# Two gate tiles in fp32 from the normalised activations at the head of a hybrid block's input projection, with h made beside them

## The chip, the cores and the metric

The kernel runs on one core of one Trainium2 chip. The metric is the device time of one execution in microseconds (us); lower is better. A profiled execution also has a span, from its first recorded instruction to its last, and the numbers of the trace count from the start of that span.

## The reference, cut to what matters

One layer works on 1024 tokens of width 1024, all in float32:

```python
mod = silu(c) @ ada_w + ada_b                  # 3072 numbers for the one sequence
shift, scale, gate = split(mod, 3)
h = rms_norm(x, norm_w) * (1 + scale) + shift
proj = h @ w_in                                # columns: q,k,v,z,beta,decay | q,k,v,z | g_A,g_B
y_A = (headwise_norm(gated_delta_rule(q, k, v)) * silu(z_A)) @ P_A      # 8 heads, 16 chunks of 64
y_B = (dilated window attention * silu(z_B)) @ P_B                      # 12 heads in 3 groups
x = x + gate * ((sigmoid(g_A) * y_A + sigmoid(g_B) * y_B) @ w_out)
out = rms_norm(x, final_norm_w)
```

With xn for x divided by its root mean square, and A = norm_w * (1 + scale), the first line of the block is h = A * xn + shift. A column w of the input projection is therefore h @ w = xn @ (A * w) + shift @ w. The two forms of this equation are the kernel before and a part of the change.

## The kernel before, in words

Everything on chip is held transposed, with features on the 128 partitions and the 1024 tokens along the free axis. h is eight such tiles (`hT[kk]`, kk from 0 to 7). The program multiplies in two ways. A plain float32 matmul is issued as two instructions. The large products use a split instead: each operand is written as hi + lo in the type float32r, and three products (hi by hi, hi by lo, lo by hi) are added up in PSUM. One output tile of the projection, 128 features by 1024 tokens, so takes 8 kk x 3 products x 2 halves of 512 tokens = 48 matmuls of 128x512.

The order of all instructions is set before the kernel runs. Each piece of work is a Python generator (a stream) with a priority; `Sched.run` steps the streams with a rough clock of its own, and what they issue lands in each engine's queue in that order. On the chip every engine runs its queue strictly in order and waits for what it needs. The projection is the stream of lowest priority (99): it fills TensorE wherever the others wait by that clock. A buffer comes from a pool of slots (`big` has 34 tiles of 128x1024); `get(add=...)` makes a projection tile wait until enough slots are left, so a tile of the attention (kinds qB, add=4) can be held back while the recurrence holds its buffers, where a gate tile (add=0) is not.

The head of the kernel, all before the first steady stretch, is this:

- SyncE (SP) issues the loads in the order of `LOADS`: the eight tiles of x, then pairs of ada_w tiles (scale tile 8+kk with shift tile kk) and the halves of the first two weight tiles.
- `ln_start`: ScalarE squares and sums a tile of x, VectorE adds eps, GpSimd takes the power -0.5, VectorE multiplies the tile by it in place.
- `consts_start` broadcasts c over the partitions with a float32 matmul and applies SiLU, into the SBUF tile `scb[0]`.
- `ada_stream`: for each kk two products with sum on VectorE (`ada_dot`, 128x1024 each, both inputs in SBUF), an addition of the bias, and A_d[kk].
- `h_stream`: for each kk and half, four transposes on TensorE, then two ScalarE passes with scale A_d and bias shift (one to hi, one to a float32 scratch), then on GpSimd lo = scratch - hi.
- `projections`, streams `first`: the first two tiles (k of heads 0 and 1, called k0 and k1 here) take each kk as it comes; all later tiles run whole.

After the head comes the gated delta rule in four pairs of heads. Its recurrence (`rec_stream`) is a serial chain over 8 steps: the state products kt*st and qt*st, VectorE, the product with `tt`, a ScalarE copy, the products kp*w and at*w, VectorE again. The matmuls are 128x128 in plain float32, and two heads run in step. Between them TensorE runs the projection's matmuls. The list `ORDER` says which projection tiles come while which pair runs; a "g" in it takes the next of 16 gate tiles.

```python
    for g_ in range(3):
        for i_ in (0, 1):
            feat("qB", 2 * g_ + i_)
            feat("kB", 2 * g_ + i_)
```

These follow `ORDER`, then six zB tiles, then gate tiles that are left, and then the output products.

Of the kernel before, what the change touches and what calls it, by code (L numbers as in the profile page):

```python
# [21 lines left out]
LOADS = "s x0 s x1 s x2 s x3 x4 x5 x6 x7 a0 w00 w10 a1 a2 a3 w01 a4 a5 a6 a7 w11"  # L22
LAG = 2
FIRST = 2
INFLIGHT = 4
# [25 lines left out]
class Slots:  # L51
# [201 lines left out]
def hybrid_block_kernel(ctx: ExitStack, tc: tile.TileContext, x, c, norm_w, ada_w, ada_b, w_tiles, w_vb0, w_vb1,  # L253
# [82 lines left out]
    def load_start():  # L336
        for u in units[0:FIRST]:
            u.raw = yield from (big if u is units[2] else wr).get(shape=[P, u.n])
            u.half_raw, u.half_ev = [Event(), Event()], [Event(), Event()]
# [3 lines left out]
        for o in LOADS.split():  # L343
# [11 lines left out]
            else:  # L355
                kk = int(o[1])
                if kk >= INFLIGHT:
                    yield ada_ev[kk - INFLIGHT]
                yield from ada_fetch(kk)
# [39 lines left out]
    def consts_start():  # L399
# [7 lines left out]

        for hf in range(2):
            pb = yield from sb.get()
            pe.matmul(pb, one_row, scb[1][0:1, hf * 512:(hf + 1) * 512], start=True, stop=True)  # L410
            yield
            if hf == 0:
                scb[0] = yield from big.get()
            act.activation(scb[0][:, hf * 512:(hf + 1) * 512], pb, AF.Silu)
            sb.put()
        big.put()
        S.set(ev_mod)

    def ln_start():
        junk = yield from big.get()  # L420
        live = [8]

        def one(i):
# [21 lines left out]
    ada_ev = [Event() for _ in range(24)]  # L445

    def ada_dot(j, aw):
        mdt = yield from big.get()
        dve.scalar_tensor_tensor(mdt, aw, 1.0, scb[0], op0=OP.mult, op1=OP.mult, accum_out=mod[:, j:j + 1])
        dve.tensor_tensor(mod[:, j:j + 1], mod[:, j:j + 1], adab[:, j:j + 1], op=OP.add)  # L450
        big.put()

    def ada_stream():
        for kk in range(8):
            yield ev_mod
            for j in (8 + kk, kk):
                yield ev_aw[j]
                yield from ada_dot(j, aw[j])
                big.put()
            dve.scalar_tensor_tensor(A_d[:, kk:kk + 1], mod[:, 8 + kk:9 + kk], 1.0, nw_t[:, kk:kk + 1],  # L460
                                     op0=OP.add, op1=OP.mult)
            S.set(ada_ev[kk])
        yield ev_k[1]
        for j in range(16, 24):
# [3 lines left out]
            yield from ada_dot(j, a_)  # L468
# [5 lines left out]
    todo_h = []  # L474
    for k_ in range(8 + LAG):
        todo_h += [(kk, hf) for hf in range(2) for kk in [k_ - LAG * hf] if 0 <= kk < 8]
    h_left = [16]

    def h_stream():
        while todo_h:  # L480
            kk, hf = todo_h.pop(0)
            h32 = yield from mid.get()
# [5 lines left out]
            yield ada_ev[kk]
            if kk not in hT:
                hT[kk] = None  # L490
                hi = yield from big.get(F32R)
                lo = yield from big.get(F32R)
                hT[kk] = (hi, lo)
            yield lambda: hT[kk] is not None
            hi, lo = hT[kk]
            sl = slice(hf * 512, hf * 512 + 512)
# [32 lines left out]
    def w_split():  # L529
        yield lambda: hasattr(units[FIRST - 1], "half_raw")  # L530
        for u in units[0:FIRST]:
            u.pool = big if u is units[2] else wh
            u.hi = yield from u.pool.get(F32R, shape=[P, u.n])
            u.lo = yield from u.pool.get(F32R, shape=[P, u.n])
        for q in range(2):
            for u in units[0:FIRST]:
                yield u.half_raw[q]
                sl = slice(q * 512, q * 512 + 512)
# [1184 lines left out]
```

## Time and profile before

| | |
|---|---|
| median of 3 runs | 1302.04 us (1301.1 to 1302.54) |
| the profiled execution | 1300.81 us, its span 1299.0 us |
| TensorE (PE) busy | 1261.6 us, 97% of the span |
| VectorE (DVE) busy | 690.9 us, 53% |
| ScalarE (ACT) busy | 494.3 us, 38% |
| GpSimd (POOL) busy | 145.4 us, 11% |
| DMA | 137.65 MB, 106 GB/s on average |

The rows of the trace name an operation by the tiles that it writes and reads: `pj` are the PSUM tiles of the projection, `sb` the small PSUM tiles, `wr` raw weights, `wh` split weights, `mid` scratch of 128x512, `mod` the 24 columns of shift, scale and gate. L96 is the helper that records every instruction, so the rows are told apart by tiles and times. A row of the timeline has its start, its length, engine, operation, out<-in, shapes and how many instructions are merged in it; in brackets stands the idle time before it and what ended that. PEld is TensorE's weight load, which overlaps the matmuls; a plain float32 matmul shows as two instructions in the trace.

### The profile page before, as it was taken

Reading aid. Unit: us, or ns where it says so; the run is one execution under the profiler, and the core shown is the slowest. Engines: PE = TensorE matmul, PEld = TensorE weight load, DVE = VectorE, ACT = ScalarE, POOL = GpSimd, SP = SyncE. Lnnn points to the kernel's source line nnn. Section 1 sums busy time; section 2 is a strip of 40 time slices with the busy share of each in tenths; the row PEclk is TensorE's granted clock in tenths of the full one; section 3 lists DMA queues with packets and bytes.
Section 4 is the critical chain, followed back from the end, with each engine's and each line's share of the span. In section 5 each row is a group of like instructions: output and inputs, shape, how many; then the busy total and the mean of one; then the engine's idle time right before and its main releaser. Section 6 shows DMA issues by size and latency. Waiting matters only on the chain.

```text
span 1299.0 us, 18858 instructions
## 1 busy us (share of the span) xinstructions
PE 1261.6 (97%) x7386; PEld 1049.0 (81%) x7386; DVE 690.9 (53%) x1437; ACT 494.3 (38%) x1054; POOL 145.4 (11%) x97
## 2 busy tenths in 40 slices
PE   5799899999999999999999999999999999999997
PEld 3698678988888988888888888777777888888886
DVE  6766682377763468843778533232322147645433
ACT  5637312455234362234542242453536342222211
POOL 4601200023000221001310002000000000002400
PEclk9899999999999999999999999999999999999999
DMA  9335532163321433231522226211100257333422
GB/s 362 120 123 179 95 93 58 33 197 94 95 70 40 149 125 93 78 102 33 179 74 73 82 66 194 66 35 65 35 33 33 83 187 208 102 127 117 156 95 89
DMA packets 76138, 137.65 MB, mean 106 GB/s; under 512 B 30193, under 2 KB 43921, under 8 KB 76050
## 3 DMA queue, kind: packets, MB, share of 16 engines
q1 hardware_dynamic: 75906, 136.20, 33.2%
q8 instruction: 58, 0.95, 0.3%
q14 instruction: 30, 0.25, 0.1%
q10 hardware_dynamic: 144, 0.26, 0.1%
HBM read 105.84 MB, written 30.59 MB: 105 GB/s over the span
## 4 chain that ended last, share of the span: by engine, by line
PE 82%; issue 7%; DVE 6%; DMA 3%; POOL 1%; ACT 1%; SPq 0%; POOLq 0%; DVEq 0%; ACTq 0%
PE pj L96 69%; PE sb L96 13%; DVE big L96 4%; DMA big<-in_x_dram 1%; DMA vtd<-big 1%; DVE wh L96 1%; POOL big L96 1%; DVE mod L96 1%; DMA big<-grow 0%; ACT big L96 0%; DVE mid L96 0%; DMA big<-otd 0%; SPq L96 0%; POOL mo L96 0%; DMA otd<-big 0%
## 5 line engine op out<-in xcount | busy, mean ns | idle before, releaser
L96 PE MATMUL pj<-big,wh 128*128 128x512 f32 x3840 | 941.8, 398 | 11.2 <-POOL big L96 6.4
L96 PEld LDWEIGHTS pj<-big,wh 128*128 128x128 f32 x3840 | 706.3, 189 | 157.5 <-POOL big L96 7.8
L96 ACT ACTIVATE wh<-wr 128x1024 fp32r<-128x1024 f32 (+3 forms) x96 | 95.6, 996 | 316.1 <-PE pj L96 292.4
L96 DVE TENSOR_TENSOR wh<-wr,wh 128x1024 fp32r<-128x1024 f32 (+3 forms) x93 | 115.5, 1243 | 148.1 <-ACT wh L96 147.9
L96 ACT ACTIVATE big<-big 128x1024 f32<-128x1024 f32 (+1 forms) x61 | 64.5, 1059 | 147.2 <-DVE big L96 115.7
L96 PE MATMUL pj<-wh,big 128*128 128x256 f32 (+2 forms) x702 | 109.5, 307 | 0.0
L96 PEld LDWEIGHTS pj<-wh,big 128*128 128x128 f32 x702 | 95.9, 189 | 5.2 <-DVE big L96 0.2
L96 DVE SCALAR_TENSOR_TENSOR big<-pj,cw,big 128x1023 f32<-128x1023 f32 (+2 forms) x66 | 84.4, 1279 | 1.8 <-ACT big L96 0.3
L96 PEld LDWEIGHTS sb<-sq,big 128*128 128x128 f32 x464 | 62.6, 191 | 4.4
L96 PE MATMUL sb<-sq,big 128*128 128x128 f32 x464 | 65.5, 274 | 0.0
L96 DVE TENSOR_TENSOR big<-big,big 128x1024 f32<-128x1024 f32 (+3 forms) x40 | 55.2, 1388 | 15.1 <-ACT big L96 13.0
L96 ACT ACTIVATE big<-pj 128x1024 f32<-128x1024 f32 (+1 forms) x56 | 51.7, 923 | 21.3 <-PE pj L96 21.2
L96 ACT ACTIVATE mid<-sb 128x384 f32<-128x384 f32 (+5 forms) x75 | 34.1, 461 | 66.8 <-PE sb L96 66.4
L96 POOL TENSOR_TENSOR wh<-wr,wh 128x1024 fp32r<-128x1024 f32 x3 | 8.4, 2785 | 399.0 <-ACT wh L96 399.0
L96 ACT ACTIVATE mid<-mid,sta 128x128 f32<-128x128 f32 (+1 forms) x96 | 42.2, 441 | 25.5 <-DVE sta L96 25.4
L96 DVE COPY big<-sb 128x256 f32<-128x256 f32 (+1 forms) x32 | 12.4, 389 | 74.0 <-PE sb L96 73.9
L96 DVE SCALAR_TENSOR_TENSOR sq<-sq,gsm,sb 128x128 f32<-128x128 f32 x48 | 16.5, 345 | 63.2 <-PE sb L96 61.8
L96 PE MATMUL pj<-big,big 128*128 128x512 f32 x210 | 49.1, 389 | 0.0
L96 ACT ACT_TABLE_LOAD x29 | 37.2, 1283 | 28.8 <-DVE big L96 23.9
L96 PE MATMUL sb<-big,big 128*128 128x128 f32 (+4 forms) x365 | 45.5, 316 | 2.0 <-DVE big L96 2.0
L96 PEld LDWEIGHTS pj<-big,big 128*128 128x128 f32 x210 | 39.4, 188 | 8.2
L96 DVE TENSOR_TENSOR mid<-big 64x31 f32<-64x31 f32 (+15 forms) x124 | 41.1, 332 | 9.0 <-POOL big L96 5.6
(124 smaller groups left out, 1086.3 us busy)
## 6 DMA issues: line engine op xcount, KB each, us to landing
wr<-in_w_tiles_dram SPq DMA_DIRECT2D x64, 512.0 KB, 3.9
big<-in_ada_w_dram SPq DMA_DIRECT2D x24, 512.0 KB, 9.0
big<-in_x_dram SPq DMA_DIRECT2D x16, 512.0 KB, 5.0
gd<-big SPq DMA_DIRECT2D x16, 512.0 KB, 5.0
big<-gd SPq DMA_DIRECT2D x16, 512.0 KB, 4.7
big<-grow SPq DMA_DIRECT2D x8, 512.0 KB, 5.6
vtd<-big SPq DMA_DIRECT2D x8, 512.0 KB, 3.0
big<-vtd SPq DMA_DIRECT2D x32, 128.0 KB, 3.8
```

Source lines behind the costliest of these rows:

```text
L96: r = f(*a, **k)
```

## The change

The list of tiles begins with two gate tiles (`gA` 0 and 1, called g0 and g1 here) instead of k0 and k1; k0 and k1 come third and fourth, as ordinary split tiles. Two gate tiles fewer are left for `ORDER` and the end. g0 and g1 are computed in plain float32 from xn: the transposed xn is kept in SBUF (`XT`, a ScalarE copy of the transposes), the raw weights are multiplied by A_d on GpSimd (`u.ws`), and each tile is 16 float32 matmuls of 128x512 instead of 48 split ones. shift enters as sixteen matmuls with one column (`mod` against the raw weights), whose result is the bias `fb` of the tanh. The loads bring the eight scale tiles (e0 to e7) first and the eight shift tiles (f0 to f7) behind them. silu(c) now stays in PSUM for the sixteen dots, which are one custom VectorE instruction with the bias added in. h is made from XT: hi by one ScalarE pass of 1024, the float32 values by two VectorE passes of 512, lo on GpSimd as before.

```diff
-LOADS = "s x0 s x1 s x2 s x3 x4 x5 x6 x7 a0 w00 w10 a1 a2 a3 w01 a4 a5 a6 a7 w11"
+LOADS = "s x0 s x1 s x2 s x3 w00 w10 e0 e1 x4 e2 x5 e3 x6 w01 e4 w11 x7 e5 e6 e7 f0 f1 f2 f3 f4 f5 f6 f7"
-INFLIGHT = 4
+INFLIGHT = 5
...
     def consts_start():
...
+        pb = yield from pj.get()
         for hf in range(2):
-            pb = yield from sb.get()
-            pe.matmul(pb, one_row, scb[1][0:1, hf * 512:(hf + 1) * 512], start=True, stop=True)
...
+            pe.matmul(pb[:, hf * 512:hf * 512 + 512], one_row, scb[1][0:1, hf * 512:hf * 512 + 512], start=True, stop=True)
+        yield
+        act.activation(pb, pb, AF.Silu)
+        scb[2] = pb
+        S.set(ev_mod)
+        yield
+        scb[0] = yield from big.get()
+        act.activation(scb[0], pb, AF.Copy)
...
     def ada_dot(j, aw, cc):
         mdt = yield from big.get()
-        dve.scalar_tensor_tensor(mdt, aw, 1.0, scb[0], op0=OP.mult, op1=OP.mult, accum_out=mod[:, j:j + 1])
-        dve.tensor_tensor(mod[:, j:j + 1], mod[:, j:j + 1], adab[:, j:j + 1], op=OP.add)
+        dve.tensor_tensor_reduce(mdt, aw, cc, 1.0, adab[:, j:j + 1], op0=OP.mult, op1=OP.add, accum_out=mod[:, j:j + 1])
...
+        for n, j in enumerate([8, 9, 10, 11, 12, 13, 14, 15, 0, 1, 2, 3, 4, 5, 6, 7]):
+            yield ev_aw[j]
+            yield from ada_dot(j, aw[j], scb[2])
...
+            if n < 8:
+                dve.tensor_scalar(A_d[:, n:n + 1], mod[:, j:j + 1], 1.0, nw_t[:, n:n + 1], op0=OP.add, op1=OP.mult)
...
+    def xt_stream():
...
+            for i in range(4):
+                pe.transpose(pb[:, i * P:(i + 1) * P], xs[4 * hf + i][:, kk * P:(kk + 1) * P], ident)
...
+            act.activation(XT[kk][:, hf * 512:hf * 512 + 512], pb, AF.Copy)
...
     def h_stream():
...
-            act.activation(hi[:, sl], pb, AF.Identity, bias=mod[:, kk:kk + 1], scale=A_d[:, kk:kk + 1])
-            act.activation(h32, pb, AF.Identity, bias=mod[:, kk:kk + 1], scale=A_d[:, kk:kk + 1])
...
-            pool.tensor_tensor(lo[:, sl], h32, hi[:, sl].bitcast(F32), op=OP.subtract)
+            act.activation(hi, XT[kk], AF.Identity, bias=mod[:, kk:kk + 1], scale=A_d[:, kk:kk + 1])
+            for q in range(2):
+                sl = slice(q * 512, q * 512 + 512)
+                dve.tensor_scalar(ts[q], XT[kk][:, sl], A_d[:, kk:kk + 1], mod[:, kk:kk + 1], op0=OP.mult, op1=OP.add)
+            yield
+            for q in range(2):
+                sl = slice(q * 512, q * 512 + 512)
+                pool.tensor_tensor(lo[:, sl], ts[q], hi[:, sl].bitcast(F32), op=OP.subtract)
...
+    def first_weights():
...
+            for u in units[0:FIRST]:
+                pool.tensor_tensor(u.ws[:, ks], u.raw[:, ks], A_d[:, kk:kk + 1].to_broadcast([P, P]), op=OP.mult)
+            S.set(ev_ws[kk])
+        yield ev_sh
+        pb = yield from sb.get()
+        for q, u in enumerate(units[0:FIRST]):
+            for kk in range(8):
+                pe.matmul(pb[:, q:q + 1], u.raw[:, kk * P:kk * P + P], mod[:, kk:kk + 1], start=kk == 0, stop=kk == 7)
+        wh.put(2)
+        yield
+        dve.tensor_scalar(fb, pb[:, 0:2], 0.5, None, op0=OP.mult)
...
+    gate_tile()
+    gate_tile()
     feat("kA", 0)
     feat("kA", 1)
...
         def first(q, hf):
...
-                pe.matmul(o, u.hi[:, ks], hi[:, sl], start=kk == 0, stop=False)
-                pe.matmul(o, u.hi[:, ks], lo[:, sl], start=False, stop=False)
-                pe.matmul(o, u.lo[:, ks], hi[:, sl], start=False, stop=kk == 7)
+                pe.matmul(o, u.ws[:, kk * P:kk * P + P], XT[kk][:, sl], start=kk == 0, stop=kk == 7)
```

How this moves instructions is shown at three places. The first is TensorE's queue at the end of the head. Before, it goes from the last split matmuls of k1 (`pj_235`) straight to the third tile, q of head 0 (`pj_634`, weights `wh_559` and `wh_560`):

```order
L96 MATMUL pj_235<-big_519,wh_231 128x512
L96 MATMUL pj_235<-big_547,wh_230 128x512
L96 MATMUL pj_235<-big_548,wh_230 128x512
L96 MATMUL pj_235<-big_547,wh_231 128x512
L96 MATMUL pj_634<-big_304,wh_559 128x512 x2
L96 MATMUL pj_634<-big_305,wh_559 128x512 x2
```

With the change, g0 is `pj_224`, the second half of g1 is `sb_227`, and the third tile, `pj_596`, is k0. `sb_531` is the product for the bias, and it reads all eight shift columns of `mod`:

```order
L103 MATMUL pj_224<-big_342,wh_221 128x512
L103 MATMUL pj_224<-big_347,wh_221 128x512
L103 MATMUL sb_227<-big_263,wh_222 128x512
L103 MATMUL sb_531<-mod,wh_183 128x1 x8
L103 MATMUL sb_531<-mod,wh_184 128x1 x8
L103 MATMUL sb_227<-big_268,wh_222 128x512
L103 MATMUL sb_227<-big_287,wh_222 128x512
L103 MATMUL sb_227<-big_290,wh_222 128x512
L103 MATMUL sb_227<-big_315,wh_222 128x512
L103 MATMUL sb_227<-big_321,wh_222 128x512
L103 MATMUL sb_227<-big_342,wh_222 128x512
L103 MATMUL sb_227<-big_347,wh_222 128x512
```

The bias product stands ahead of the last seven float32 matmuls of g1 and of k0, which come right behind it.

The second place is VectorE's queue around the last shift dots of the change. A row "ISA" is the dot (f5, f6 and f7 here, each followed by its sum into `mod`); the rows into `mid` are the float32 values of h for kk = 3 (`big_290`), 4 and 5:

```order
L103 ISA big_488,mod<-big_409,pj_228,adab 128x1024
L103 ISA mod 128x1
L103 TENSOR_SCALAR mid_492<-big_290,A_d,mod 128x512
L103 TENSOR_SCALAR mid_493<-big_290,A_d,mod 128x512
L103 ISA big_499,mod<-big_428,pj_228,adab 128x1024
L103 ISA mod 128x1
L103 ISA big_502,mod<-big_453,pj_228,adab 128x1024
L103 ISA mod 128x1
L103 TENSOR_SCALAR mid_508<-big_315,A_d,mod 128x512
L103 TENSOR_SCALAR mid_509<-big_315,A_d,mod 128x512
```

Eight of the sixteen passes into `mid` (kk = 0 to 3) stand ahead of the last dot, and eight behind it.

The third place is TensorE's queue in the last steps of the recurrence of the last pair of heads (`TT_100`, `TT_101`; `sb<-sq` are the state products). Before, every step has projection matmuls between its parts:

```order
L96 MATMUL sb_6792<-sq_6782,TT_101 128x128
L96 MATMUL pj_6711<-big_451,wh_6307 128x512 x2
L96 MATMUL sb_6796<-sq_6787,TT_100 128x128
L96 MATMUL pj_6711<-big_452,wh_6307 128x512 x2
L96 MATMUL sb_6804<-sq_6798,big_5725 128x128
L96 MATMUL sb_6804<-sq_6798,big_5543 128x128
L96 MATMUL sb_6807<-sq_6802,big_5621 128x128
L96 MATMUL sb_6807<-sq_6802,big_5454 128x128
L96 MATMUL pj_6711<-big_451,wh_6308 128x512 x2
L96 MATMUL pj_6711<-big_481,wh_6307 128x512 x2
L96 MATMUL sb_6821<-sq_6810,big_5538 128x128
L96 MATMUL sb_6821<-sq_6810,big_6044 128x128
```

With the change, the same step of the same two heads reads:

```order
L103 MATMUL sb_6833<-sq_6827,TT_101 128x128
L103 MATMUL sb_6835<-sq_6830,TT_100 128x128
L103 MATMUL sb_6841<-sq_6837,big_5792 128x128
L103 MATMUL sb_6841<-sq_6837,big_5610 128x128
L103 MATMUL sb_6844<-sq_6839,big_5688 128x128
L103 MATMUL sb_6844<-sq_6839,big_5521 128x128
L103 MATMUL sb_6854<-sq_6847,big_5605 128x128
L103 MATMUL sb_6854<-sq_6847,big_6111 128x128
L103 MATMUL sb_6858<-sq_6850,big_5516 128x128
L103 MATMUL sb_6858<-sq_6850,big_5694 128x128
```

Three steps in a row are without any projection matmul there. In this stretch 52 of 62 projection matmuls are gone, and 4 of them come back in the block behind it; the other 48 that leave the later part of the queue stood in the long run of projection and output matmuls ahead of and in the output products. Between the head and this stretch the queue keeps its order, apart from blocks whose ends shift by two to four matmuls, and behind it too.

More of the change, by code (lines that the diff above doesn't have):

```diff
@@ L70, in get, with many @@
         return self.pool.tile(shape or self.shape, dtype, tag=self.tag, name=f"{self.tag}{self.count}")
+    def many(self, n):
+        yield lambda: len(self.free_at) >= n
+        ts = []
+        for _ in range(n):
+            ts.append((yield from self.get()))
+        return ts
     def put(self, n=1, t=None):
@@ L355, in load_start @@
             else:
[L356 to L359, printed above, removed]
+                n, j = len(aw), int(o[1]) + (8 if o[0] == "e" else 0)
+                if n >= INFLIGHT:
+                    yield ev_dot[n - INFLIGHT]
+                aw[j] = yield from big.get()
+                restart()
+                sp.dma_start(aw[j], ada_w[j * P:(j + 1) * P, :])
+                S.set(ev_aw[j])
         ev_loaded.t = S.now()
@@ L472, in ada_stream @@
         big.put()
[L474 to L482, printed above, removed]
+    todo_x = [(kk, hf) for hf in range(2) for kk in range(8)]
+    x_left = [8, 8]
+    def xt_stream():
+        while todo_x:
+            kk, hf = todo_x.pop(0)
             yield [ev_ln[hf], ev_const]
@@ L486, in h_stream @@
                 pe.transpose(pb[:, i * P:(i + 1) * P], xs[4 * hf + i][:, kk * P:(kk + 1) * P], ident)
+            x_left[hf] -= 1
+            if not x_left[hf]:
+                big.put(4)
             yield
[L488 to L495, printed above, removed]
@@ L496, in h_stream @@
[L496 to L498 removed]
+            if kk not in XT:
+                XT[kk] = None
+                XT[kk] = yield from big.get()
+            yield lambda: XT[kk] is not None
+            act.activation(XT[kk][:, hf * 512:hf * 512 + 512], pb, AF.Copy)
             sb.put()
[L500 removed]
@@ L529, in w_split @@
     def w_split():
[L530 to L538, printed above, removed]
-                act.activation(u.hi[:, sl], u.raw[:, sl], AF.Copy)
-                yield
-                dve.tensor_tensor(u.lo[:, sl], u.raw[:, sl], u.hi[:, sl].bitcast(F32), op=OP.subtract)
-                S.set(u.half_ev[q])
-                if q:
-                    (big if u is units[2] else wr).put()
         for u in units[FIRST:]:
@@ L636, in hybrid_block_kernel, with first_out @@
     GT = {}
+    def first_out(q, j, pt):
+        t = GT[j]
+        for hf in range(2):
+            act.activation(t[:, hf * 512:hf * 512 + 512], pt[hf], AF.Tanh, bias=fb[:, q:q + 1], scale=0.5)
+        (pj if q < 1 else sb).put(1 + q)
+        yield
+        sp.dma_start(gate_d[j], t)
+        S.set(ev_gate[j])
+        big.put()
     prog = []
```

119 lines of the change are left out of this document (66 added, 53 removed).

## The prediction

> **What bounds the kernel now.** I read the page first, its busy times and slices.
>
> ```profile
> PE 1261.6 (97%) x7386; PEld 1049.0 (81%) x7386; DVE 690.9 (53%) x1437; ACT 494.3 (38%) x1054; POOL 145.4 (11%) x97
> PE   5799899999999999999999999999999999999997
> ```
>
> TensorE is the bound from the third slice on; 37 us of idle are left, and the first two slices hold most. So I cut the trace into stretches (stretch, length, then busy of PE, PEld, DVE, ACT, POOL, the granted clock, DMA share, GB/s).
>
> ```profile
> 0.00:22.00 22.00, 9.00 (x20) 4.25 (x20) 10.55 (x28) 13.54 (x23) 8.74 (x16) 1.00 0.91 341
> 22.00:44.00 22.00, 15.99 (x71) 11.94 (x71) 21.65 (x36) 12.50 (x19) 14.59 (x8) 1.00 0.88 332
> 44.00:66.00 22.00, 18.54 (x75) 14.60 (x76) 12.27 (x19) 13.41 (x19) 12.83 (x9) 0.84 0.13 38
> 100.00:200.00 100.00, 93.28 (x456) 77.50 (x455) 71.78 (x162) 40.38 (x77) 14.04 (x8) 0.98 0.46 121
> 700.00:800.00 100.00, 100.00 (x710) 84.65 (x709) 49.94 (x107) 34.97 (x90) 8.33 (x5) 1.00 0.30 89
> ```
>
> From 22 to 44 us VectorE is busy 21.65 of 22 us, so it paces the head, with the loads (332 GB/s) ahead of it; later on TensorE has no gap, as from 700 to 800 us. The timeline shows how the head ends.
>
> ```profile
> 47.89 1.21 DVE L96 SCALAR_TENSOR_TENSOR big<-big,big 128x1024 f32<-128x1024 f32 x1
> 49.03 0.07 DVE L96 DVE_READ_ACCUMULATOR big<-big,big 128x1 f32 x1
> 49.14 1.12 DVE L96 TENSOR_TENSOR mod<-mod,adab 128x1 f32<-128x1 f32 x1
> 53.88 0.15 DVE L96 SCALAR_TENSOR_TENSOR A_d<-mod,nw_t 128x1 f32<-128x1 f32 x1
> 55.63 2.63 POOL L96 TENSOR_TENSOR big<-mid,big 128x512 fp32r<-128x512 f32 x2 [1.70 <-ACT mid L96]
> 76.58 14.45 PE L96 MATMUL pj<-wh,big 128*128 128x272 f32 x114
> ```
>
> The last scale column is ready at 53.88, lo follows on GpSimd, and the fourth tile of the program (values, 128x272 products) begins at 76.58: then k0, k1 and q of head 0, three tiles, are done. **My sum compares this instant with the one at which g0, g1 and k0 are done.** Behind it both queues hold the same number of projection matmuls in almost the same order.
>
> **The change part by part.** First the prices.
>
> ```profile
> 1252.21 0.55 POOL L96 TENSOR_TENSOR fss<-fss,pw 128x1 f32<-128x1 f32 x1 [10.33 <-DVE fss L96]
> 1263.09 0.55 POOL L96 TENSOR_TENSOR fss<-fss,pw 128x1 f32<-128x1 f32 x1 [10.33 <-DVE fss L96]
> 312.06 3.57 PE sb L96 x32
> 109.82 0.78 PE L96 MATMUL sb<-gsm,cst 128*128 128x64 f32 x6
> 163.92 0.25 PE L96 MATMUL sb<-qpart,cst 128*32 128x8 f32 x8 [4.74 <-DVE qpart L96]
> L96 DVE CUSTOM_DVE_ANT_0 mid<-sb,cst 128x256 f32<-128x256 f32 x44 | 17.4, 420 | 8.3 <-PE sb L96 8.2
> L96 DVE CUSTOM_DVE_ANT_0 mid<-sb,cst 128x128 f32<-128x128 f32 x52 | 13.2, 288 | 15.5 <-PE sb L96 15.5
> L96 DVE TENSOR_SCALAR big<-big,rstd 128x1024 f32<-128x1024 f32 x8 | 6.0, 753 | 4.0 <-POOL rstd L96 4.0
> L96 POOL TENSOR_TENSOR big<-mid,big 128x512 fp32r<-128x512 f32 x16 | 27.4, 1720 | 15.5 <-ACT mid L96 15.4
> 1196.40 2.41 POOL L96 TENSOR_TENSOR big<-wr,big 128x1024 fp32r<-128x1024 f32 x1 [4.99 <-PE pj L96]
> 1196.44 1.22 DVE L96 SCALAR_TENSOR_TENSOR big<-big,pj 128x1024 f32<-128x1024 f32 x1 [1.53 <-PE pj L96]
> 1197.70 2.20 DVE L96 TENSOR_TENSOR big<-big,big 128x1024 f32<-128x1024 f32 x1
> ```
>
> A split tile of 48 matmuls takes 1263.09 - 1252.21 = 10.9 us. Sixteen plain float32 matmuls of 128x128 take 3.57 us, 0.223 each, so one of 128x512 about 0.9 (estimate, four times the columns), and a gate tile 16 x 0.9 = 14.4 us. The two dearer tiles alone would lose 2 x (14.4 - 10.9) = 7.0 us; the gain must come from starting earlier.
>
> *Dot.* The custom instruction with one PSUM input grows by 132 ns per 128 elements: 288 + 7 x 132 = 1.21 us at 1024, and with its sum I take a pitch of 1.3. The bias addition of the old form (1.12 above, mostly waiting) is gone. A VectorE instruction with a PSUM input ran its 1.22 us in full beside a GpSimd one (1196.44 against 1196.40), while one with two SBUF inputs then took 2.20. So I let the dots run free beside lo. [...]
>
> *Start.* The fourth tile of x was normalised from 12.49 to 13.24.
>
> ```profile
> 5.41 1.06 ACT L96 ACTIVATE big<-big 128x1024 f32<-128x1024 f32 x1 [0.34 <-DMA big<-in_x_dram]
> 6.37 0.19 ACT L96 ACTIVATION_READ_ACCUMULATOR big<-big 128x1 f32 x1
> 10.32 1.06 ACT L96 ACTIVATE big<-big 128x1024 f32<-128x1024 f32 x1 [0.16 <-DMA big<-in_x_dram]
> 12.49 0.75 DVE L96 TENSOR_SCALAR big<-big,rstd 128x1024 f32<-128x1024 f32 x1 [0.66 <-POOL rstd L96]
> 2.40 3.75 PE L96 MATMUL sb<-big,one_row 1*128 1x512 f32 x4 [2.40 <-DMA big<-in_c_dram]
> ```
>
> Now ScalarE's SiLU waits for both broadcast matmuls (2.40 + 3.75 = 6.15) and takes about 1.1 in one piece, so the first square starts near 7.4 instead of 5.41. A square with its sum takes 1.15 (5.41 to 6.56), and a copy of 1.0 stands between them, so the fourth starts at 7.4 + 3 x 1.15 + 1.0 = 11.85 instead of 10.32, and the normalisation ends 1.5 later: 14.7.
>
> *Scale phase.* VectorE does 8 dots (10.4), 8 A_d (0.8), four normalisations (4 x 0.75) and their small parts (0.6), and I add 0.6 of waits: 15.4, ending at 30.1. The loads cover this: e7 is complete at 9.5 MB, and at the rates above 7.5 MB are in by 22 us, so it lands at 22 + 2.0 / 0.332 = 28.0.
>
> *Shift phase, to the last dot.* 8 dots are 10.4; the eight passes of 512 ahead of it cost, by 753 ns for 1024, between 0.38 and 0.75 each; I take 0.45, 3.6. Each may wait for a running lo, between nothing and 1.3 (half of the 2.63 for two lo at 55.63); I take 0.45, 3.6. End: 30.1 + 17.6 = 47.7. f7 lands at 40.7 (13.7 MB), so nothing waits for the loads.
>
> *TensorE behind it.* Ahead of the bias it has 25 float32 matmuls (22.5) and 64 transposes (at 0.11, 7.1) from about 16.6 on, when the first dot and its weights are through: 46.2. So it **waits about 1.5 us for the bias**, with seven matmuls of g1 and all of k0 queued behind. Sixteen one-column products are 32 instructions, between 0.03 (163.92: 8 in 0.25) and 0.13 each (109.82: 6 in 0.78); I take 0.06, 1.9 us. Then 7 x 0.9 = 6.3 and k0's 10.9: 47.7 + 19.1 = 66.8.
>
> ```profile
> 44.55 1.17 PE L96 MATMUL pj<-big,wh 128*128 128x512 f32 x2 [2.28 <-POOL big L96]
> 46.22 2.48 PE L96 MATMUL pj<-big,wh 128*128 128x512 f32 x6
> 37.79 1.64 PE L96 MATMUL pj<-big,wh 128*128 128x512 f32 x6
> ```
>
> After an idle of 2.28 six matmuls took 2.48 instead of 1.64 us, so I add 1.0: **67.8, and the head gains 76.6 - 67.8 = 8.8 us.** [...]
>
> *lo on GpSimd.* Sixteen lo at the mean of 1.72 take 27.5 from about 35: 62.5. k0 needs the last one near 66.4, so they are covered by 3.9 us; beyond that k0 waits for lo one for one. The sixteen products for `u.ws` (128x128, about 0.4 by a quarter of lo) lie in the scale phase, where GpSimd is mostly idle. ScalarE loses 32 passes of 512 and gains 16 copies of 512 and 8 passes of 1024, and it was busy 12.5 of 22 us: no cost. k0's weights are loaded behind f7 and split on ScalarE and VectorE (1.2 each) beside g1's last matmuls; the bytes loaded stay the same.
>
> *The recurrence without its filler.* A full step of both heads today:
>
> ```profile
> 770.45 1.06 PE L96 MATMUL sb<-sq,big 128*128 128x128 f32 x8
> 771.17 0.73 DVE L96 SCALAR_TENSOR_TENSOR sq<-sb,gsm,big 128x128 f32<-128x128 f32 x2 [0.89 <-PE sb L96]
> 772.27 0.38 PE L96 MATMUL sb<-sq,TT 128*128 128x128 f32 x2
> 772.69 0.28 ACT L96 ACTIVATE sq<-sb 128x128 f32<-128x128 f32 x1 [0.38 <-PE sb L96]
> 773.64 1.05 PE L96 MATMUL sb<-sq,big 128*128 128x128 f32 x8
> 774.28 0.35 DVE L96 SCALAR_TENSOR_TENSOR sq<-sq,gsm,sb 128x128 f32<-128x128 f32 x1 [2.38 <-PE sb L96]
> 777.27 0.38 PE L96 MATMUL sb<-sq,TT 128*128 128x128 f32 x2
> ```
>
> It is 5.0 long (772.27 to 777.27), full of TensorE work: ten recurrence matmuls (2.3) and twelve fillers (2.7). Bare, only the chain counts: 0.72 to VectorE, 0.36 there, 0.42 to ScalarE, 0.28 there, 0.64 to VectorE, 0.35 there, and about 0.1 for each return to TensorE: 3.0. TensorE idles 3.0 - 2.3 = 0.7 in each of three bare steps, with the half-bare ends about **3.0 us lost** (nearer 1 if the hops overlap better, 10.9 = 48 x 0.227 if a bare step stays at 5.0).
>
> *Sum:* -8.8 + 3.0 = -5.8, so the profiled execution goes from 1300.81 (its span 1299.0) to 1295.0; it lay 1.2 below the median of 1302.04, and against the median the change gives 1296.2, **1296 us**. The idle of 6.7 from 100 to 200 us stays, since that stretch keeps its order.
>
> **The rivals.**
>
> (A) *h is not made beside the gates.* The passes into `mid` and lo take turns and each pass waits nearly a whole lo: 8 x 0.9 instead of 0.45 adds 3.6, and lo ends later too. The head gains 5.2, and 5.2 - 3.0 leaves 1299.8: no change that shows. For it: GpSimd then works without a break, and the row at 1197.70; against it: during every free dot GpSimd can finish a lo. If all the waits come in full (1.3 each, 6.8 more), it is 1303.0.
>
> (B) *Slower: the recurrence of the last pair.* The bare step stays near 5.0, because ScalarE's and VectorE's other work (weight splits, of 1 us and more) falls into its hops. Then 10.9 is lost: 1302.04 - 8.8 + 10.9 = 1304.1. It decides from a bare step of about 4.9 on, where three steps of (4.9 - 2.3) and 0.9 at the ends eat the 8.8. Against it: the hops add up to 3.0, and TensorE set today's 5.0.
>
> (C) *More gain:* TensorE finds the shift ready at 46.2 and keeps its clock; with 19.1 k0 ends at 65.3, the gain is 11.3, and with 1.0 lost in the recurrence the time is 1291.7. It needs passes without waits.
>
> **How the numbers follow.** My forecast, a change of -2.6 to -9 us, has 0.54; A 0.18; B 0.12; C 0.13; 0.03 is left for no effect by other chances. About 0.2% (2.6 us) is what a measurement of this kernel tells from no change. Faster: 0.54 + 0.13 of C + 0.03 of A = 0.70. Same: 0.13 of A + 0.03 = 0.16. Slower: 0.02 of A + 0.12 = 0.14. The forecast's own range is 1293 to 1299.4; over the cases it is 1290 to 1303.
>
> **What would show it.** Right: the last shift dot ends near 48, TensorE's gap stands ahead of `sb<-mod`, the 128x272 products begin two tiles behind 67.8, dots of 1.2 to 1.3 beside lo, and bare steps of 3.0 with 2 to 4 us more idle in the last pair. Wrong: passes into `mid` of a microsecond and more (A), bare steps of 5 (B), a float32 512-wide matmul far from 0.9, or a new gap behind 100 us.

## The result, and the profile after

| | before | after |
|---|---|---|
| median | 1301.57 us (1300.77 to 1302.54) | 1286.78 us (1286.06 to 1287.35, 4 runs) |
| ratio to before | | 0.9886, 95% interval 0.9869 to 0.9903 |
| the profiled execution, its span | 1300.81 us, 1299.0 us | 1286.06 us, 1284.3 us |

The change wins 14.8 us. The forecast was 1296.0, a gain of 5.8, with a range of 1293 to 1299.4 (1290 to 1303 over all its cases). The result lies below both: the direction was right, the size was not.

Two lines of the page of the changed kernel, the busy times and TensorE's slices:

```profile
PE 1264.3 (98%) x7386; PEld 1044.5 (81%) x7386; DVE 688.9 (54%) x1426; ACT 485.6 (38%) x1042; POOL 148.5 (12%) x113
PE   7999999999999999999999999999999999999997
```

The second slice has filled. The same stretches as before, with the same columns (stretch, length, busy time of PE, PEld, DVE, ACT, POOL, granted clock, DMA share, GB/s):

```profile
22.00:44.00 22.00, 22.00 (x86) 12.09 (x85) 19.36 (x36) 15.12 (x23) 13.63 (x18) 1.00 0.92 362
44.00:66.00 22.00, 21.91 (x98) 15.70 (x97) 17.38 (x18) 7.74 (x9) 16.54 (x11) 1.00 0.35 111
100.00:200.00 100.00, 99.28 (x540) 85.25 (x539) 72.30 (x163) 41.67 (x80) 13.99 (x8) 1.00 0.37 114
700.00:800.00 100.00, 98.63 (x693) 82.25 (x692) 49.96 (x109) 34.52 (x89) 8.33 (x5) 1.00 0.31 95
```

TensorE is full from 22 us on. From 700 to 800 us it now has gaps, as forecast. But from 100 to 200 us it is busy 99.28 instead of 93.28 us, which was not forecast. The timeline gives two instants that cut the run into stages: the first 128x272 product (values of the first group) and the first 128x256 product (the second group). First the second instant of the kernel before (the prediction quotes its first one, 76.58), then the rows of the changed kernel:

```profile
231.21 1.67 PE L96 MATMUL pj<-wh,big 128*128 128x256 f32 x12
```

```profile
54.99 33.23 PE L103 MATMUL pj<-big,wh 128*128 128x512 f32 x144
88.06 6.17 PE L103 MATMUL pj<-wh,big 128*128 128x272 f32 x48
234.81 1.68 PE L103 MATMUL pj<-wh,big 128*128 128x256 f32 x12
```

k0, k1 and q0 are the 144 matmuls from 54.99 to 88.06, 11.02 us each, so three tiles of the program are done at 66.0. The two tiles that now stand ahead of the first instant (88.06 - 66.01 = 22.05 us) are missing behind the second. With them put back:

| stage | before | after | gain | forecast |
|---|---|---|---|---|
| head, to three tiles done | 76.6 | 66.0 | 10.6 | 8.8 |
| first 128x272 to first 128x256 | 154.6 | 146.8 | 7.9 | 0 |
| first 128x256 to the end | 1067.8 | 1049.5 + 22.05 | -3.75 | -3.0 |
| sum | 1299.0 | 1284.3 | 14.7 | 5.8 |

Each column is one profile. In the other profiles below, three tiles are done at 76.3 to 77.8 with the head of the kernel before and at 65.8 to 67.1 with the changed one, so a difference of 1 us in one stage says little.

The head and the recurrence came out near their forecast, and a third term, larger than the whole forecast, was set to zero. What differs there shows in the DMAs of that stretch (timeline of SP's queue: start, length, DMA; then the list of DMA issues: KB each, median us from issue to landing) and in what VectorE waits for. Before:

```profile
130.30 0.37 SPq L96 DMA_DIRECT2D rowd<-mod  x1
132.17 0.32 SPq L96 DMA_DIRECT2D vtd<-big  x1
...
vtd<-big SPq DMA_DIRECT2D x1, 512.0 KB, 11.3
rowd<-mod SPq DMA_DIRECT2D x1, 4.0 KB, 12.2
...
148.70 1.23 DVE L96 TENSOR_TENSOR big<-big,ik 128x1024 f32<-128x1024 f32 x1 [9.16 <-DMA big<-vtd]
```

After:

```profile
132.09 0.37 SPq L103 DMA_DIRECT2D rowd<-mod  x1
145.53 0.32 SPq L103 DMA_DIRECT2D vtd<-big  x1
...
vtd<-big SPq DMA_DIRECT2D x1, 512.0 KB, 2.8
...
141.01 2.63 DVE L103 TENSOR_TENSOR_SCAN big<-big,cst 128x128 f32<-128x128 f32 x8 [5.32 <-DMA big<-grow]
153.41 1.23 DVE L103 TENSOR_TENSOR big<-big,ik 128x1024 f32<-128x1024 f32 x1 [0.50 <-DMA big<-vtd]
168.63 0.25 PE L103 MATMUL sb<-qpart,cst 128*32 128x8 f32 x8 [0.72 <-DVE qpart L103]
```

`rowd<-mod` is the last line of `ada_stream`: the 1024 numbers of the output gate go to DRAM transposed, in 1024 pieces of four bytes. It takes 12.2 us for 4 KB in the kernel before. There, the bounce of head 0's values (`vtd<-big`, the first half of `turn`) is issued 1.9 us behind it and lands after 11.3 us instead of 2.8; VectorE, in order, waits 9.16 us, and TensorE runs dry behind it (the 4.74 that the prediction quotes is one of three waits). In the changed kernel the bounce comes 13.4 us behind the store and goes free; the store now delays a load of `grow` instead, issued 4.5 us ahead of it (it lands after 13.4 us, and VectorE waits 5.32 us for it), while TensorE has projection work. That is a reading of two traces; the experiments test it.

### The profile page after: what moved, and what is told of

It is laid out like the page before. It is cut to its first block, busy times and chain, and to the rows that moved or that the text cites. A ratio compares the mean times of both kernels' runs of the same rounds, so it can differ in the third digit from the quotient of the medians.

```text
span 1284.3 us, 18871 instructions
## 1 busy us (share of the span) xinstructions
PE 1264.3 (98%) x7386; PEld 1044.5 (81%) x7386; DVE 688.9 (54%) x1426; ACT 485.6 (38%) x1042; POOL 148.5 (12%) x113
## 4 chain that ended last, share of the span: by engine, by line
PE 83%; issue 7%; DVE 5%; DMA 2%; ACT 1%; POOL 1%; SPq 0%; POOLq 0%; DVEq 0%; ACTq 0%
PE pj L103 69%; PE sb L103 14%; DVE big L103 3%; DMA big<-grow 1%; ACT big L103 1%; DVE mid L103 1%; DVE wh L103 1%; POOL big L103 1%; ACT wh L103 0%; DMA big<-otd 0%; DMA big<-vtd 0%; POOL mo L103 0%; DMA otd<-big 0%; DMA vtd<-big 0%; SPq L103 0%
## 5 line engine op out<-in xcount | busy, mean ns | idle before, releaser
L103 PE MATMUL pj<-big,wh 128*128 128x512 f32 x3776 | 922.7, 397 | 0.0
L103 PEld LDWEIGHTS pj<-big,wh 128*128 128x128 f32 x3776 | 692.9, 188 | 145.8 <-issue 11.0
L103 ACT ACTIVATE wh<-wr 128x1024 fp32r<-128x1024 f32 (+2 forms) x92 | 93.2, 1013 | 314.1 <-PE pj L103 300.7
L103 DVE TENSOR_TENSOR wh<-wr,wh 128x1024 fp32r<-128x1024 f32 (+2 forms) x89 | 114.2, 1284 | 145.0 <-ACT wh L103 144.8
L103 DVE SCALAR_TENSOR_TENSOR big<-pj,cw,big 128x1023 f32<-128x1023 f32 (+2 forms) x72 | 92.0, 1278 | 1.7
L103 ACT ACTIVATE big<-pj 128x1024 f32<-128x1024 f32 (+1 forms) x53 | 48.6, 917 | 18.4 <-PE pj L103 18.3
L103 POOL TENSOR_TENSOR mo<-mo,pw 128x8 f32<-128x8 f32 x8 | 13.1, 1636 | 283.4 <-DVE mo L103 283.3
```

Source lines behind the costliest of these rows:

```text
L103: r = f(*a, **k)
```

## The experiments

All times are medians; each run stands beside runs of the kernel before (1300.8 to 1301.3 us).

**The store, moved.** Theory T1: the store holds up the bounce. T2: VectorE's lighter load or new order does it.

```diff
         dve.tensor_scalar(mod[:, 16:24], mod[:, 16:24], 0.5, None, op0=OP.mult)
-        sp.dma_start(row_d.rearrange("o (j p) -> p (o j)", p=P), mod[:, 16:24])
         big.put()
+        yield ev_qb[3]
+        sp.dma_start(row_d.rearrange("o (j p) -> p (o j)", p=P), mod[:, 16:24])
```

Every other engine keeps its order, and so does SP's queue but for this one DMA. In the kernel before:

> The kernel before, with one DMA moved: the 4 KB store rowd<-mod (1024 pieces of four bytes, issued at 130.30 just ahead of the v turn of head 0) goes to SP's queue some 150 DMAs later. T1 (the 6 us of TensorE idle between 100 and 200 us come from this store holding up vtd<-big of head 0): vtd<-big lands in 2.4 to 3.0 us instead of 11.31, VectorE's wait of 9.16 ahead of the product with ik is gone, TensorE's busy time from 100 to 200 us rises from 93.28 to 98 or more, and the time falls by 5 to 6.5 us, to 1295 to 1296.5. T2 (the idle comes from the order or load of VectorE, which the change lightened): no change, 1300.5 to 1302.5, and the idle stays at 6 to 7.

Measured: 1291.22 us, ratio 0.9926 (0.9913 to 0.9938), 9.5 us faster. The bounce in the list of DMA issues, VectorE's row behind it, the stretch, and the two instants:

```profile
vtd<-big SPq DMA_DIRECT2D x1, 512.0 KB, 2.7
...
141.62 1.22 DVE L96 TENSOR_TENSOR big<-big,ik 128x1024 f32<-128x1024 f32 x1 [0.98 <-DMA big<-vtd]
100.00:200.00 100.00, 100.00 (x501) 84.29 (x500) 74.37 (x167) 41.49 (x78) 14.04 (x8) 1.00 0.40 127
...
77.82 14.45 PE L96 MATMUL pj<-wh,big 128*128 128x272 f32 x114
223.35 1.67 PE L96 MATMUL pj<-wh,big 128*128 128x256 f32 x12
```

The landing and the wait came as T1 said, and T1 holds. Its time was too high, 1295 to 1296.5, because the collision costs more than its 6.7 us of recorded idle: the second stage goes from 154.6 to 223.35 - 77.82 = 145.5 us. In the kernel before the granted clock over that stretch is 0.98, here 1.00; by an estimate, 2% of 100 us would make up most of the rest. In the changed kernel:

> The changed kernel with the same single move of rowd<-mod. T1: in the changed kernel the store meets no v turn, but the load big<-grow issued just before it, which lands after up to 13.4 us while TensorE has filler work; so that landing falls to some 3 us and VectorE's wait of 5.32 at 141 goes, but of the time at most TensorE's 0.72 of idle: 1286 to 1287. T2: no change either. If instead the time falls by more than 1 us, the collision with grow costs TensorE work that the idle column does not show.

Measured: 1286.53, ratio 0.9888 (0.9874 to 0.9901), no difference from 1286.78, and VectorE's wait of 5.32 us for `grow` is gone. With the store out of the way in both kernels, **the change itself is worth 1291.22 - 1286.53 = 4.7 us**, near the forecast 5.8.

**The store, brought back.** The changed kernel, with the store tied to the bounce. Its two lines go from `ada_stream`, which sets `ev_row2` at its end, to `turn`:

```diff
     def turn(src, dst, bounce):
...
         yield
+        if bounce is vt_d[0]:
+            yield ev_row2
+            dve.tensor_scalar(mod[:, 16:24], mod[:, 16:24], 0.5, None, op0=OP.mult)
+            sp.dma_start(row_d.rearrange("o (j p) -> p (o j)", p=P), mod[:, 16:24])
         sp.dma_start(bounce, t)
```

> The changed kernel with the store brought into the collision: the small VectorE instruction that halves the gate columns is queued behind the stream transpose of head 0's v turn, so rowd<-mod is issued right ahead of vtd<-big, as in the kernel before. T1: vtd<-big lands after about 11 us instead of 2.4 to 2.9, VectorE waits about 9 us for it, TensorE idles 4 to 6 us more between 100 and 200 us, and the time is 1290.5 to 1293. T2: no change, 1286 to 1287.5.

Measured: 1295.16, ratio 0.9953 (0.9939 to 0.9966), 8.4 us slower than the changed kernel: T1, and again a larger loss than it gave (1290.5 to 1293). The late landing and the waits of the kernel before are back (list of DMA issues, then timeline):

```profile
vtd<-big SPq DMA_DIRECT2D x1, 512.0 KB, 11.9
...
161.19 1.23 DVE L103 TENSOR_TENSOR big<-big,ik 128x1024 f32<-128x1024 f32 x1 [8.71 <-DMA big<-vtd]
176.40 0.29 PE L103 MATMUL sb<-qpart,cst 128*32 128x8 f32 x8 [4.99 <-DVE qpart L103]
```

This is the changed kernel as the prediction imagined it, its head better and its stretch from 100 to 200 us as before (TensorE busy for 93.08 us of it); it takes 1295.2 where 1296.0 was forecast.

**The store from another queue.** In the kernel before, `sp.dma_start` of this store becomes `act.dma_start` at the same place.

> The kernel before with rowd<-mod issued from ScalarE's DMA queue at the same place of the program instead of SP's. Q (the store holds up vtd<-big because both stand in SP's queue, one behind the other): the v turn lands in 2.4 to 3 us and the time falls by 8 to 9.5 us, to 1291 to 1293, as with the moved store. E (the 1024 four-byte pieces keep the DMA engines themselves busy, whichever queue they come from): vtd<-big still takes about 11 us and the time stays at 1300 to 1302.

Measured: 1301.14, ratio 1.0004 (0.9995 to 1.0013): no difference. The store now has a queue of its own, and the bounce on SP's is as late as ever (list of DMA issues):

```profile
vtd<-big SPq DMA_DIRECT2D x1, 512.0 KB, 11.3
rowd<-mod ACTq DMA_DIRECT2D x1, 4.0 KB, 12.5
```

So it is not the place in the queue: E's time and landing came, and another queue does not help. What the DMA engines do meanwhile shows in three stretches (columns as above): the bounce in flight in the kernel before, the bounce and the transfers behind it in the kernel with the moved store, and the changed kernel while VectorE waits for `grow` (until 141.01).

```profile
132.00:142.00 10.00, 10.00 (x62) 8.87 (x61) 7.16 (x13) 6.30 (x7) 7.67 (x4) 1.00 0.96 58
134.00:138.00 4.00, 4.00 (x23) 3.47 (x22) 3.93 (x4) 0.76 (x1) 4.00 (x2) 1.00 0.82 289
135.00:141.00 6.00, 6.00 (x29) 4.95 (x28) 0.59 (x4) 5.85 (x14) 3.51 (x2) 1.00 0.02 1
```

In the first the engines count as busy (0.96) and move 58 GB/s, in the second 289: the bounce's data themselves are late. In the third next to nothing moves (1 GB/s), and in the 4 us behind it nothing (0 GB/s from 141 to 145 us), so by these records the data of `grow` are through, and VectorE waits for its landing all the same. By what means the store slows the data in the first and holds up the landing in the third, and why a second queue does not help, no run here tells.

**The dots alone.** The kernel before, with silu(c) in PSUM and the new dot, and nothing else of the change (`consts_start` becomes that of the change, and k1's output takes small PSUM tiles, since silu(c) holds a large one):

```diff
...
-        dve.scalar_tensor_tensor(mdt, aw, 1.0, scb[0], op0=OP.mult, op1=OP.mult, accum_out=mod[:, j:j + 1])
-        dve.tensor_tensor(mod[:, j:j + 1], mod[:, j:j + 1], adab[:, j:j + 1], op=OP.add)
+        dve.tensor_tensor_reduce(mdt, aw, cc, 1.0, adab[:, j:j + 1], op0=OP.mult, op1=OP.add, accum_out=mod[:, j:j + 1])
...
```

> The kernel before with one part of the change alone: silu(c) stays in PSUM and the sixteen dots are the custom VectorE instruction with the bias added in (pitch 1.27 instead of two instructions of 2.3 in all); tile order, loads, h and the first two tiles k0 and k1 stay as before (k1's PSUM tiles come from the small pool). H1 (cheap dots are what frees the head; the gate tiles made from xn add little): the last scale column is ready at 43 to 45 instead of 53.88, bound by the loads, and the 128x272 products begin at 64 to 68 instead of 76.58, so the time falls by 8 to 12 us, to 1290 to 1293.5. H2 (TensorE can start early only on work that does not need the shift and lo): lo on GpSimd, 16 x 1.72 = 27.5 us behind dots that end as late as the loads allow, holds k0 and k1; the products begin at 72 or later and the time falls by 4 us at most, to 1297.5 or more.

Measured: 1284.15, ratio 0.9869 (0.9856 to 0.9883): 16.6 us faster than before, and 2.6 faster than the whole change. From its timeline, the last scale column, the first instant, and the two DMAs:

```profile
44.04 0.60 DVE L96 SCALAR_TENSOR_TENSOR A_d<-mod,nw_t 128x1 f32<-128x1 f32 x1
66.88 13.69 PE L96 MATMUL pj<-wh,big 128*128 128x272 f32 x108
112.90 0.37 SPq L96 DMA_DIRECT2D rowd<-mod  x1
130.72 0.32 SPq L96 DMA_DIRECT2D vtd<-big  x1
```

H1 holds: the last scale column is ready at 44.6 and three tiles are done at 66.9, 9.7 us earlier than before. The rest of the change brings the head to 66.0, 0.9 better in these two profiles and so less than one head varies between profiles, and then costs the last pair its filler. My time for this run was 6 to 9 us too high, for the reason of the prediction itself: I left the collision where it was, but the store comes 17.8 us ahead of the bounce here, and the second stage takes 144.8 us. Of the 981 matmul instructions of that stage 18 fell behind its end in this kernel, so a part of that is only moved: the third stage is 2.3 us longer than before (1070.1). Moving the store as well adds nothing:

> The kernel before with the new dots alone (1284.15) and with the store moved. C1 (what the dots alone won came from the head, 9.7 us, and from a store that no longer meets a v turn, so that little of the collision is left): 1282.5 to 1284, and TensorE's busy time from 100 to 200 us near 100 instead of 98.73. C2 (the store still costs this kernel some 5 to 9 us that the idle column does not show): 1275 to 1279.

Measured: 1284.99, ratio 0.9874 (0.9859 to 0.9889): C1, though 1 us above its range and without the busy time near 100 (it stays at 98.73).

**Dots from SBUF.** The changed kernel, with `scb[0]` (the SBUF copy) in place of `scb[2]` (PSUM) in the sixteen dots, and the copy ahead of them.

> The changed kernel with the sixteen dots reading silu(c) from its SBUF copy instead of PSUM (the copy on ScalarE comes first, about 1 us). D1 (the PSUM input is what lets the dots run beside lo and the other GpSimd work; with two SBUF inputs VectorE and GpSimd take turns, as in the row where such an instruction took 2.20 instead of 1.22): the eight shift dots take 1.7 to 2.3 us each instead of 1.27, the last ends at 51 to 56 instead of 47.2, the bias product and everything behind it comes later by as much, and the time rises by 4 to 9 us, to 1291 to 1296. D2 (the dots run at 1.27 whatever their inputs): only the copy ahead of the first square counts, and the time rises by at most 1 us.

Measured: 1297.86, ratio 0.9977 (0.9968 to 0.9987), 11.1 us slower than the changed kernel. Its timeline, a dot ahead of the first lo (which starts at 36.98), the last dot, beside lo, and then TensorE:

```profile
33.60 1.28 DVE L103 CUSTOM_DVE_ANT_0 big<-big,big,adab 128x1024 f32<-128x1024 f32 x1
51.99 2.28 DVE L103 CUSTOM_DVE_ANT_0 big<-big,big,adab 128x1024 f32<-128x1024 f32 x1
54.34 4.00 PE L103 MATMUL sb<-mod,wh 128*128 128x1 f32 x18 [2.75 <-DVE mod L103]
98.97 1.28 PE L103 MATMUL pj<-wh,big 128*128 128x272 f32 x9
```

D1, with a loss 2 us above its range: a dot from SBUF takes 1.28 us ahead of lo and 2.28 beside it, where one from PSUM takes 1.27. TensorE waits 2.75 for the shift, its granted clock from 44 to 66 us falls to 0.77, and three tiles are done at 98.97 - 22.05 = 76.9. The head's gain is gone (76.6 before).

**The bias product left out.** This kernel lacks the part of the shift in its first two gate tiles.

> The changed kernel without the sixteen one-column products for the bias: fb is set to zero, so the part shift @ w of the first two gate tiles is left out. It measures what the bias product costs. N1 (its 3.73 us on TensorE, 45.57 to 49.30, lie on the path in full): the time falls by 3.5 to 3.8, to about 1283. N2 (lo on GpSimd takes over as the bound: the last lo ends at 62.5 and its product in k0 would then start at 60.9): it falls by 1.5 to 2.5 only, and k0 shows a wait for GpSimd of 1 to 2 us. N3 (the instructions were long because they waited for the last dot): it falls by less than 1.5 and TensorE waits elsewhere for VectorE.

Measured: 1282.02, ratio 0.9856 (0.9843 to 0.987), 4.5 to 4.8 less than the changed kernel with and without the moved store: N1, and about 1 us more. Between the profiles, 3.8 of it lie in the head (first 128x272 product at 84.29 for 88.06) and 0.8 in the second stage. What else the product can cost shows in the changed kernel with the moved store, whose head is the same program and ran a little otherwise (timeline, then the stretch):

```profile
46.35 2.17 PE L103 MATMUL sb<-mod,wh 128*128 128x1 f32 x18 [0.22 <-DVE mod L103]
48.38 7.95 PE L103 MATMUL sb<-big,wh 128*128 128x512 f32 x14
44.00:66.00 22.00, 21.78 (x92) 15.20 (x91) 16.44 (x16) 6.80 (x8) 16.02 (x10) 0.92 0.34 111
```

TensorE waited 0.22 for the last dot, and the next seven float32 matmuls took 7.95 instead of the 6.25 us that they take in the changed kernel's profile, at a granted clock of 0.92 over the stretch. That clock is 1.00 in the changed kernel's profile, where no such wait shows, and without the bias product. Which of the two is the rule over many executions, these profiles do not tell.

**The bare steps of the last pair.** The second row of `ORDER` gives up a gate tile, so that the fourth row has four again:

```diff
-    "k0 k1 q0 v0 z0 g v1 q1 z1 g g B2",
+    "k0 k1 q0 v0 z0 g v1 q1 z1 g B2",
```

> The changed kernel with one gate tile moved: ORDER's second row gives up a g, so that the fourth row has its four gate tiles again and no step of any pair's recurrence is without projection matmuls. From the traces, the stretch from the first 128x256 product to the end takes 1049.5 us in the changed kernel and, with two gate tiles of 10.9 added, 1071.3 against 1067.8 before: 3.4 us lost. R1 (the three bare steps of the last pair cost these 3 to 3.4 us, as forecast): the time falls by 3 us or a little more, to 1283 to 1284, and TensorE has no idle from 750 to 800 us. R2 (they cost only the 1.37 us that the idle column shows): it falls by 1.4, to about 1285.3. R3 (the loss lies elsewhere in the tail, or the second pair now loses what the fourth gains): no change, 1286 to 1287.5.

Measured: 1286.76, ratio 0.9902 (0.9885 to 0.9919), no gain, which is R3's time; the five runs spread from 1285.4 to 1291.3. The stages tell why: the second one took 149.5 us, where the program is the same as in the changed kernel (146.8), and the third 1046.3 instead of 1049.5. In the second, TensorE's wait for `qpart` is 1.72 instead of 0.72 us, VectorE waits 5.21 for `grow` as in the changed kernel, and the granted clock from 100 to 200 us is 0.98, where the changed kernel has 1.00. So the store went along:

> The changed kernel with both moves: the store rowd<-mod goes to a late place of SP's queue, and ORDER's second row gives up a g so that the fourth pair's recurrence keeps its filler. With the store alone moved it is 1286.53. S1 (the bare steps cost 3.0 to 3.4 us, and the run with the moved gate tile alone lost as much again to a chance meeting of DMAs between 100 and 200 us): 1283 to 1283.7, with runs close together again. S2 (moving the gate tile wins nothing in sum): 1286 to 1287.

Measured: **1282.44, ratio 0.9857 (0.9842 to 0.9872)**: S1, half a microsecond below its range. It is the lowest median of the complete kernels here, 4.3 us below the changed one and 4.1 below the moved store alone. The stretch of the fourth pair, and the second instant:

```profile
700.00:800.00 100.00, 100.00 (x710) 84.62 (x709) 44.61 (x97) 34.87 (x89) 8.33 (x5) 1.00 0.34 101
...
233.73 1.68 PE L103 MATMUL pj<-wh,big 128*128 128x256 f32 x12
```

The gaps from 700 to 800 us are gone, and with a span of 1280.1 us the third stage takes 1046.4 instead of 1049.5: the filler brings back 3.1 us, where the idle column showed 1.37 (100 - 98.63).

**Loads in another order.** On the kernel with the new dots and the moved store: `LOADS` brings the first weights and the first ada_w pairs ahead of x4 to x7. The diff is that of the first form; the second brings a1 ahead of x4 too, and has LAG = 3 (the halves of the tokens three kk apart instead of two).

```diff
-LOADS = "s x0 s x1 s x2 s x3 x4 x5 x6 x7 a0 w00 w10 a1 a2 a3 w01 a4 a5 a6 a7 w11"
+LOADS = "s x0 s x1 s x2 s x3 w00 a0 w10 x4 a1 x5 a2 x6 x7 a3 w01 a4 w11 a5 a6 a7"
```

> The same kernel (new dots, moved store) with the loads in another order: the halves of the first weights and the first pair of ada_w tiles come before the second four tiles of x, the next pairs between them. In the kernel with the new dots the first projection product starts at 22.87, when all eight tiles of x are in and normalised. L (that start is what holds the head): it moves to 15 to 17, the 128x272 products start at 61 to 63 instead of 66.88, and the time falls by 3.5 to 6 us against the run beside it. M (the last ada_w tiles, which land at the same instant as before, or VectorE's work hold the head): less than 1.5 us.

> As the run before, with two pairs of ada_w tiles ahead of the second four tiles of x, and the two halves of the tokens three kk apart instead of two, so that TensorE has more products of the first half while the second is loaded. L: a start at 15 to 17 too, fewer gaps of TensorE between 16 and 30 us, the 128x272 products at 60 to 63. M: as above, no more than 1.5 us. If it is slower than the run before, the second half of x has become what TensorE waits for.

Measured: 1283.21, ratio 0.9862 (0.9848 to 0.9877), and 1285.55, ratio 0.9883 (0.9866 to 0.9899), beside 1284.99. The first form wins 1.8 us, the second loses 0.6: nearer to M (under 1.5) than to L (3.5 to 6), and hardly clear of the spread of the runs (1283.45 to 1285.39 beside them). The first product moves from 22.87 to 17.87 and 17.84, but three tiles are done at 67.5 and 68.7 (66.9 and 68.1 with the old order). TensorE only waits more often in between (timeline of the first form), and its granted clock from 22 to 44 us is 0.92 in both forms, 1.00 with the old order; how much of the lost gain is the clock stays open:

```profile
32.81 1.13 PE L96 MATMUL pj<-big,wh 128*128 128x512 f32 x2 [1.23 <-POOL big L96]
```

## Why the prediction was right or wrong

**The step that failed** is this sentence: "The idle of 6.7 from 100 to 200 us stays, since that stretch keeps its order." The engines' order did stay, the distances in time did not. The store waits for VectorE's gate columns, the bounce for head 0's values; what VectorE did in between changed, and 1.9 us of distance became 13.4. The prediction had the 4.74 of waiting in a fence, as the price of a small matmul, and did not ask what it waited for. The lost wait was worth 7.9 of the 14.7 us; moved by hand it is 9.1 (154.6 to 145.5). No rival had it either.

**The head**, 10.6 for 8.8. Several terms were off, and partly cancel. The timeline of the changed kernel, TensorE with the last dot between:

```profile
44.71 1.02 PE L103 MATMUL sb<-big,wh 128*128 128x512 f32 x2
45.57 3.88 PE L103 MATMUL sb<-mod,wh 128*128 128x1 f32 x32
45.94 1.27 DVE L103 CUSTOM_DVE_ANT_0 big<-big,pj,adab 128x1024 f32<-128x1024 f32 x1
49.30 6.25 PE L103 MATMUL sb<-big,wh 128*128 128x512 f32 x14
```

- The wait of 1.5 for the bias is missing: the product begins at 45.57, right behind its predecessor, and its first instructions run while the last dot ends (45.94 + 1.27 = 47.2, forecast 47.7). The forecast let the whole product wait for the last shift column, which only its eighth matmul needs first. With it went the 1.0 for the lost clock, in this profile; two other runs of the same head, with the store alone and the gate tile alone moved, have waits of 0.22 and 0.20 and lose 1.7 (7.95 for 6.25).
- The bias product, 1.9 by forecast, takes 49.30 - 45.57 = 3.73, 0.117 per instruction: the upper of the two bounds, not the value between that I took.
- A float32 matmul of 128x512 takes (54.99 - 49.30) / 7 = 0.81 to 45.57 - 44.71 = 0.86, for 0.9.

From 47.7 to k0's end I had 1.0 + 1.9 + 6.3 + 10.9, so 67.8; it was 45.57 + 3.73 + 5.69 + 11.02 = 66.0.

**The dots beside lo** ran as forecast; the end of the last one is right in part by luck (groups of VectorE's rows from 31.8 to 47.1 us, the shift phase up to the last dot: busy, mean ns):

```profile
L103 DVE CUSTOM_DVE_ANT_0 big<-big,pj,adab 128x1024 f32<-128x1024 f32 x8 | 10.0, 1274 | 0.0
L103 DVE TENSOR_SCALAR mid<-big,A_d,mod 128x512 f32<-128x512 f32 x8 | 6.0, 790 | 0.0
```

A dot took 1.27 (forecast 1.3), a pass into `mid` 0.79 where 0.45 and 0.45 of waiting made 0.9. The scale phase ended at 31.9 instead of 30.1, and the shift phase took 15.3 us instead of 17.6; the two errors cancel to 47.2 for 47.7. No row of the kernel before shows what such a pass loses beside lo, so the 0.45 of waiting was my estimate; in the changed kernel two passes took 1.00 us together where they ran mostly between two lo (at 40.71) and 2.00 mostly beside one (at 36.39). What the dots beside lo are worth was tested with the dots from SBUF: three tiles done at 76.9, against 76.6 in the kernel before and 66.0 in the changed one. Rival A needed passes of 1.35 us and did not happen.

**lo** ends where it should (GpSimd's timeline, its last two):

```profile
58.86 3.67 POOL L103 TENSOR_TENSOR big<-mid,big 128x512 fp32r<-128x512 f32 x2 [0.45 <-DVE mid L103]
```

62.5, as forecast, and TensorE never waited for it.

**The recurrence**: 3.0 forecast, 3.1 measured by giving the filler back. The rows of the bare steps:

```profile
769.10 0.75 PE L103 MATMUL sb<-sq,TT 128*128 128x128 f32 x4 [0.75 <-DVE sq L103]
769.97 2.32 PE L103 MATMUL sb<-sq,big 128*128 128x128 f32 x16
772.35 0.87 PE L103 MATMUL sb<-sq,TT 128*128 128x128 f32 x4
775.68 0.88 PE L103 MATMUL sb<-sq,TT 128*128 128x128 f32 x4
```

A step is 3.25 to 3.33 long (forecast 3.0), with 2.3 of work; by the forecast's own sum, three such steps and the ends would lose 3 x 1.0 + 0.9 = 3.9, near the 3.75 of the table. The 3.1 is what one gate tile put elsewhere wins back, net of what its old place loses. The gaps between its matmuls stand inside the lengths of these rows, not in the idle column. Rival B (a step of 5) fell. How the other 0.6 of the 3.75 divides between that net and the length put back for a tile (11.02 here, 10.9 in the prediction) stays open. Rival C had the right event, no wait for the shift, but for another reason than it gave (its passes without waits did not come), and too small a prize, since the collision was not in it.

The change's own reason holds only in part. What frees the head is the cheaper dot, which any order of tiles could have used: alone it brings 9.7 of the 10.6 us, and with dots from SBUF the rest of the change brings none.

## What to carry to other kernels

When a change shifts one stretch of a kernel against another, list the waits behind it that hang on a DMA, and ask of each what the DMA met on its way; such a wait can go or come without any instruction moved (here 9.16 us became 0.50). A store like this one (1024 pieces of four bytes, 12.2 us) belongs, by these runs, where nothing is due within the next dozen microseconds, loads issued up to 4.5 us before it included; issuing it from ScalarE's queue did not help here (the bounce took 11.3 us either way). And test the parts of a change alone: here the dot was most of the gain, and the tile order that came with it cost 3 to 4 us, of which one gate tile put elsewhere wins back 3.

## What the hardware showed

- A store of 4 KB in 1024 pieces took 12.2 us from SP's queue and 12.5 from ScalarE's, and a 512 KB transfer issued behind it (on SP's queue 0.4 and 1.9 us behind) landed after 11.3 to 11.9 us instead of 2.7 to 2.8. In the kernel before the DMA engines moved 58 GB/s meanwhile, with the store elsewhere 289. Of two 512 KB loads issued 4.9 and 4.5 us ahead of the store, the first landed after 5.1 us and the second after 13.4, though 1 GB/s was all that moved from 135 us to its landing at 141; the median of the two was 9.2 us, and 6.5 with the store moved.
- A VectorE dot of 128x1024 with both inputs in SBUF took 2.28 us beside GpSimd's lo and 1.28 ahead of it; with one input in PSUM it took 1.27 beside lo too.
- A float32 product with a single column cost TensorE 0.117 us per instruction (32 in 3.73 us). Where 0.22 us of waiting fell among 32 of them, the next seven matmuls took 7.95 instead of 6.25 us, at a granted clock of 0.92 instead of 1.00; no run here separates the wait from the products.
- Idle time in the rows of TensorE understated two losses here: 6.7 us of it cost 9.1 (with the granted clock at 0.98), and where 1.37 showed, 3.1 came back.
